# Where the gate read-back, the first weight tiles and the first gathers stand in the queues of a product-key expert layer

## The chip, the cores and the metric

The kernel runs on one core of a Trainium2 chip. The metric is device time in microseconds (us) of one launch, the median of the runs shown. TensorE is PE, VectorE is DVE, ScalarE is ACT, GpSimd is POOL, SyncE is SP; each takes its instructions in program order.

## What is computed

A decoder trunk of two layers on 512 tokens of width 1024. A layer is an attention mixer of four head groups and, behind it, an expert sub-layer of 16,384 experts, on which the change works:

```python
s1 = einsum('thd,kd->thk', q[:, :, 0], sub_k1); s2 = einsum('thd,kd->thk', q[:, :, 1], sub_k2)
v1, i1 = top_k(s1, 16); v2, i2 = top_k(s2, 16)
top_s, top_j = top_k(v1[..., :, None] + v2[..., None, :], 16)
eid = take_along_axis(i1 * 128 + i2, top_j); gate = softmax(top_s)
act = gelu(einsum('cd,ced->ce', h, u[eid]))          # 8 heads x 16 experts a token
out = einsum('ce,ced->cd', gate * act, v[eid])
x = x + g2 * out
```

## The kernel before

The 512 tokens are four tiles of 128. For the first three tiles the expert sub-layer is done densely: all 16,384 experts, in 128 blocks of 128, are multiplied on PE with 384 tokens, and a matrix of gates, zero nearly everywhere, picks the chosen ones. The fourth tile is done sparsely: for each of its 128 (head, rank) pairs a gather on POOL fetches one row of `peer_u` or `peer_v` a token, and DVE makes the dot product or the weighted sum.

Every dense product is made of three matmuls, since each operand is split into a high part (ACT copies it, rounded) and a low part (DVE or POOL subtracts). For block e these are `uh`, `ul` (from the load `ur`), `vh`, `vl` (from `vr`), and for the gated activations `wdh`, `wdl`.

The sub-layer of a layer has two stages.

**The planned stage** is put in order by `Plan`, a list scheduler with costs and due times, which writes one instruction order for each engine. It does the search for the largest scores, decodes the chosen expert numbers (`ids`, `places`, `chosen`, `decoded`, `finish`: tiles `cid`, `oh`, `ts`), and turns gates into dense blocks: DVE writes one-hot tiles `o` (L1656), scales them by the high and low part of the gates into `og` (L1669 on DVE, or L1666 on ACT for the low part, as the plan chooses), PE multiplies them (L1677), ACT evacuates into `gs` (L1683), and SP stores `gs` to DRAM as `gdram` (L1686). The u products of the first blocks run in between (`u_mm`, PE L204 to L206 on `psb`), each followed by a Gelu into a ring of `act` tiles. `QD` gives the due times of the four tiles' decoding; the fourth tile's decoding ends in `eid` and `g3`, which only the gathers and their weights need.

**The loop** over e is written by hand (from L1908 on), in the order of the code. Step e loads `ur` of block e + 33 and `vr` of block e + 3, reads back a quarter of a `gq` tile every fourth step (the gates of four blocks out of `gdram`), multiplies act by gates (`w_mul`), splits (`w_split`, `v_split`), runs `u_mm(e + 31)` and then `products(e)`, 18 matmuls into `psa`. Between them come about three uses of gathered tiles on DVE (`g_use`, L1795 and L1800), each followed by the next gather on POOL (`g_issue`, L1775). `GB` = 6 gather buffers, three buffers of `vr` and three of `ur` are in turn.

Ahead of the loop, in this order: six gathers are issued; then `v_load` of blocks 0, 1 and 2, `gq_load(0)`, `v_split(0)`, and `prepare(0)`, which is `w_mul(0)` and `w_split(0)`. PE's first product of the loop, `products(0)`, so waits for `gq`, `act`, `wdh` and `wdl` of block 0.

Of the kernel before, what the change touches and what calls it, by code (L numbers as in the profile page):

```python
# [30 lines left out]
LA = 3  # L31
PE_EPS = 0.05
SAME = 0.1
QD = (30, 70, 110, 150, 2)
GD = (45, 2.4)
UD = (0, 6.2)
QS = ((0, 30), (30, 30), (60, 34))
# [12 lines left out]
URB, VRB, GB = 3, 3, 6  # L50
# [102 lines left out]
def trunk(ctx: ExitStack, tc: tile.TileContext, I, out):  # L153
# [514 lines left out]
    for l in range(L):  # L668
# [113 lines left out]
        with tc.tile_pool(name=f"hP{l}", bufs=1) as hp, tc.tile_pool(name=f"U{l}", bufs=1) as up:  # L782
            state = peer(nc, tc, I, l, xd, fh, fl, h3, (order, qcm, hcm, ocm), q0, (wq0, wq1, wq2), both, wq_mm, right, hp, up, small, bank, mm3, iota128, cst["pos"], ident, dram, grow,
                         (ada_load, ada_mac, ada_finish, [(l, 5)] + [(l + 1, j) for j in range(2 if l + 1 < L else 0)]), l + 1 < L, lambda l=l: rows_out(l + 1))
# [543 lines left out]
def peer(nc, tc, I, l, xd, fh, fl, h3, closing, q0, w012, both, wq_mm, right, hp, up, small, bank, mm3, iota128, pos, ident, dram, grow, ada, more, rows_out):  # L1328
    V, S, G, PE, SY = nc.vector, nc.scalar, nc.gpsimd, nc.tensor, nc.sync
# [41 lines left out]
    def act_room():  # L1371
        return ring[0].tile([128, 384], F32, name="act", tag="act", bufs=RING + 1)
# [4 lines left out]
    with tc.tile_pool(name=f"Q{l}", bufs=1) as qp:  # L1377
# [7 lines left out]
        raw, w, qcs, q1, jps, tops, cands, cms = {}, dict(enumerate(w012)), {}, {}, {}, {}, {}, []  # L1385
# [178 lines left out]
        if True:  # L1564
            picked, cids, ohs, prs, turned = {}, {}, {}, {}, {}

            def weigh(i):
                tf = wp.tile([128, 16, 8], F16, name="tf", tag="tf", bufs=2)
                V.tensor_copy(tf, tj[:, i].rearrange("p h s -> p s h"))
                ge = wp.tile([128, 8, 16], F32, name="ge", tag="ge", bufs=2)  # L1570
                V.tensor_tensor(out=ge, in0=ts[:, i], in1=bc(ts[:, i, :, 0:1], [128, 8, 16]), op=ALU.subtract)
                picked[i] = (tf, ge)
# [117 lines left out]
            for i in range(NT):  # L1690
                due, d = B0 + QD[i], QD[4]
                head = t = plan.add(due, lambda i=i: weigh(i), ("W", 0.35), after=[lg[h, i] for h in range(8)] + [ready], take=("p",))
# [74 lines left out]
    def g_issue():  # L1767
        nonlocal issued
        if issued < len(events):
            kind, s = events[issued]  # L1770
            t = ep.tile([128, D], F32, name="gt", tag="gt", bufs=GB)
            if kind == "a":
                ada[0](*s, t)
            else:
                G.indirect_dma_start(out=t, out_offset=None, in_=I["peer_u" if kind == "u" else "peer_v"],  # L1775
                                     in_offset=bass.IndirectOffsetOnAxis(ap=eid3[:, s:s + 1], axis=0))
            gtile[issued] = t
            issued += 1
# [30 lines left out]
            V.tensor_mul(w3[:, r], w3[:, r], g3[:, r])  # L1809
            wdone += 1  # L1810

    for _ in range(GB):
        g_issue()

    with tc.tile_pool(name=f"D{l}", bufs=1) as dp, ExitStack() as order:
        acc = [None] * 6
        vraw, vspl, wspl, gq = {}, {}, {}, {}
# [1 line left out]
        def v_load(e):  # L1819
            if e < 128:  # L1820
                vraw[e] = up.tile([128, D], F32, name="vr", tag="ur", bufs=URB) if e >= 126 else dp.tile([128, D], F32, name="vr", tag="vr", bufs=VRB)
                SY.dma_start(vraw[e], I["peer_v"][(l * 128 + e) * 128:(l * 128 + e + 1) * 128, :])

        def gq_load(q):
            if q < 32:
                gq[q] = dp.tile([128, NTG, 4, TG], F32, name="gq", tag="gq", bufs=2)
                SY.dma_start(gq[q], gdram[:, :, 4 * q:4 * q + 4, :].rearrange("g p a t -> p g a t"))

        def w_mul(e):
            w = acts[e].rearrange("p (g t) -> p g t", g=NTG)  # L1830
            V.tensor_mul(w, w, gq[e // 4][:, :, e % 4, :])

        def w_split(e):
            w = acts.pop(e)
            if e >= 126:
                t = up.tile([128, D], F32R, name="wd", tag="ur", bufs=URB)
                wh, wl = t[:, :384], t[:, 384:768]
            else:
                wh, wl = (dp.tile([128, 384], F32R, name=q, tag=q, bufs=2) for q in ("wdh", "wdl"))
            S.activation(wh, w, AF.Copy)  # L1840
            V.tensor_sub(wl, w, wh)  # L1841
            wspl[e] = wh, wl

        def v_hi(e):
# [9 lines left out]
        def prepare(e):  # L1854
            w_mul(e)
            w_split(e)

        def v_split(e):
            v_hi(e)
            v_lo(e)  # L1860
# [37 lines left out]
        def x_add(i):  # L1898
            V.tensor_add(xs[i], xs[i], a3)

        early = {107: [(v_load, 126)], 108: [(v_load, 127)], 109: [(x_load, 3), (lambda i: grow(l, i), 5)], 110: [(v_hi, 126)], 111: [(v_lo, 126)], 112: [(v_hi, 127)], 113: [(v_lo, 127)],
                 115: [(x_mul, 3)], 116: [(x_add, 3)], 119: [(gq_load, 31)], 120: [(w_mul, 126)], 121: [(w_split, 126)], 122: [(w_mul, 127)], 123: [(w_split, 127)]}
        if more:
            for q in range(3):
# [1 line left out]
                    early.setdefault(98 + q + 3 * n, []).append((f, q))  # L1906

        order.enter_context(tc.manual_schedule())  # L1908
        for e in range(3):
            v_load(e)  # L1910
        gq_load(0)
        v_split(0)
        prepare(0)
        def a_load(e):
            acts[e] = act_room()
            SY.dma_start(acts[e], adram[e - NU])

        for e in range(125):
            if e + RING + 2 < NU:
                u_load(e + RING + 2)  # L1920
            if NU <= e + AD < 128:
                a_load(e + AD)
            if e < 123:
                v_load(e + 3)
            if e % 4 == 1 and e < 120:
                gq_load(e // 4 + 1)
            if e + RING - 1 < NU:
                u_act(e + RING - 1)
            prepare(e + 1)
            if e + RING + 1 < NU:  # L1930
                u_hi(e + RING + 1)
                u_lo(e + RING + 1, V)
            v_split(e + 1)
            for f, n in early.get(e, ()):
                f(n)
            if e + RING < NU:
                u_mm(e + RING)
            if e < 124:
                for i in range(3):
                    products(i, (e,), False)  # L1940
            upto = min(len(events), (e + 1) * len(events) // PACE)
            while used < upto:
                g_use()
                g_issue()
                g_weights()
# [195 lines left out]
```

## Time and profile before

| | |
|---|---|
| median of 3 runs | 3256.21 us (3254.5 to 3257.57) |
| the profiled execution | 3257.48 us, span of its trace 3255.7 us |
| PE busy | 3118.8 us, 96% of the span |
| DVE busy | 2576.4 us, 79% |
| ACT, POOL busy | 1329.4 us (41%), 856.1 us (26%) |
| mean granted TensorE clock | 0.984 of full speed |

The span runs from the first to the last instruction; the execution's own time has 1.8 us more around it. Busy shares are means over stages with different limits, so what one stage costs is read from its own waits.

### The profile page before, as it was taken

To read this page: it belongs to the slowest core of one execution; us is meant where nothing else is said; L and a number is where in the kernel's file an instruction comes from. 1 tells how busy PE (TensorE), PEld (TensorE's weight loads), DVE (VectorE), ACT (ScalarE), POOL (GpSimd) and SP (SyncE) were. 2 spreads that over 40 slices of the span, in tenths; PEclk is the share of its full clock that TensorE was granted. 3 is DMA by queue.
4 is the path that set the end of the run, shared out by engine and by line. 5 is a ranking of instruction groups with operands and counts; after the bars stand their busy time and mean duration, and the time that the engine had idled before them with its cause. 6 is when DMAs were issued, how large, how long until landed. Compare 5 with 4: busy or idle time off the path is not lost.

```text
span 3255.7 us, 47426 instructions
## 1 busy us (share of the span) xinstructions
PE 3118.8 (96%) x17316; PEld 2709.0 (83%) x17316; DVE 2576.4 (79%) x5530; ACT 1329.4 (41%) x2485; POOL 856.1 (26%) x694
## 2 busy tenths in 40 slices
PE   6999999989999999999989999998999999999998
PEld 5876877779989999998889678787899899999987
DVE  7757799978888888786666868999687778878856
ACT  3268414643333333333442864246333333333333
POOL 1300220024433343341022003100333444444400
PEclk9999999989999999999999999999999999999999
DMA  8502214679989999896654032146888899999954
GB/s 280 157 9 78 106 58 157 233 289 337 333 316 340 325 331 348 313 355 217 203 180 144 4 125 85 53 182 245 302 326 327 325 323 326 323 326 322 322 185 159
DMA packets 291339, 762.73 MB, mean 234 GB/s; under 512 B 23832, under 2 KB 130968, under 8 KB 285984
## 3 DMA queue, kind: packets, MB, share of 16 engines
q1 hardware_dynamic: 217376, 491.22, 43.5%
q0 software_dynamic: 73728, 268.47, 22.4%
q8 instruction: 136, 2.23, 0.3%
q14 instruction: 99, 0.81, 0.1%
HBM read 700.86 MB, written 58.74 MB: 233 GB/s over the span
## 4 chain that ended last, share of the span: by engine, by line
PE 72%; DVE 19%; DMA 4%; ACT 3%; issue 2%; POOL 0%; SPq 0%; DVEq 0%; POOLq 0%; ACTq 0%
PE psa L205 12%; PE psa L206 12%; PE psa L204 12%; PE psb L204 9%; PE psb L206 9%; PE psb L205 9%; DVE o L1656 2%; DVE og L1669 2%; PE psa L864 2%; DVE s L1457 1%; DMA wr<-in_w_in 1%; PE psa L897 1%; DMA gq<-gdram 1%; DVE ki L1455 1%; PE psa L1677 1%
## 5 line engine op out<-in xcount | busy, mean ns | idle before, releaser
L206 PE MATMUL psb<-bh,ul 128*128 128x384 f32 x1824 | 615.4, 337 | 5.2 <-DVE ul L1356 5.2
L204 PE MATMUL psb<-bh,uh 128*128 128x384 f32 x1824 | 618.6, 339 | 0.9 <-DVE arow L251 0.9
L205 PE MATMUL psb<-bl,uh 128*128 128x384 f32 x1824 | 613.5, 336 | 0.0
L204 PE MATMUL psa<-vh,wdh 128*128 128x512 f32 x1512 | 589.9, 390 | 14.5 <-ACT wdh L1840 14.5
L206 PE MATMUL psa<-vh,wdl 128*128 128x512 f32 x1512 | 593.4, 392 | 0.0
L205 PE MATMUL psa<-vl,wdh 128*128 128x512 f32 x1512 | 593.1, 392 | 0.0
L1775 POOL DMA_INDIRECT gt<-in_peer_u,eid x256 | 334.5, 1307 | 669.3 <-DVE gt L1795 235.4
L1840 ACT ACTIVATE wdh<-act 128x384 fp32r<-128x384 f32 x252 | 132.2, 524 | 866.5 <-PE psa L205 629.2
L1775 POOL DMA_INDIRECT gt<-in_peer_v,eid x256 | 324.6, 1268 | 428.3 <-DVE a L1800 199.6
L1841 DVE TENSOR_TENSOR wdl<-act,wdh 128x384 fp32r<-128x384 f32 x252 | 141.0, 559 | 284.9 <-ACT wdh L1840 274.9
L204 PEld LDWEIGHTS psb<-bh,uh 128*128 128x128 f32 x1824 | 345.0, 189 | 11.0 <-DVE arow L251 2.7
L205 PEld LDWEIGHTS psb<-bl,uh 128*128 128x128 f32 x1824 | 344.8, 189 | 8.1
L206 PEld LDWEIGHTS psb<-bh,ul 128*128 128x128 f32 x1824 | 344.3, 189 | 6.8 <-DVE ul L1356 6.8
L1356 DVE TENSOR_TENSOR ul<-ur,uh 128x1024 fp32r<-128x1024 f32 x222 | 271.9, 1225 | 91.6 <-ACT uh L1353 76.1
L204 PEld LDWEIGHTS psa<-vh,wdh 128*128 128x128 f32 x1512 | 285.1, 189 | 70.1 <-ACT wdh L1840 15.1
L206 PEld LDWEIGHTS psa<-vh,wdl 128*128 128x128 f32 x1512 | 284.6, 188 | 59.9
L205 PEld LDWEIGHTS psa<-vl,wdh 128*128 128x128 f32 x1512 | 284.6, 188 | 55.7
L1852 DVE TENSOR_TENSOR vl<-vr,vh 128x1024 fp32r<-128x1024 f32 x252 | 307.7, 1221 | 23.1 <-ACT vh L1849 22.7
L1800 DVE SCALAR_TENSOR_TENSOR a<-gt,w,a 128x1024 f32<-128x1024 f32 x254 | 325.2, 1280 | 0.8
L1795 DVE SCALAR_TENSOR_TENSOR gt<-gt,h 128x1024 f32<-128x1024 f32 x256 | 310.5, 1218 | 0.0
L1376 ACT ACTIVATE act<-psb 128x384 f32<-128x384 f32 x256 | 125.8, 491 | 394.9 <-PE psb L206 335.6
L1353 ACT ACTIVATE uh<-ur 128x1024 fp32r<-128x1024 f32 x228 | 238.7, 1047 | 91.7 <-PE psb L205 61.9
(389 smaller groups left out, 5285.7 us busy)
## 6 DMA issues: line engine op xcount, KB each, us to landing
ur<-in_peer_uT SPq DMA_DIRECT2D x256, 512.0 KB
vr<-in_peer_v SPq DMA_DIRECT2D x256, 512.0 KB
gdram<-gs SPq DMA_DIRECT2D x24, 2048.0 KB
gq<-gdram SPq DMA_DIRECT2D x64, 768.0 KB
O<-in_ada_w SPq DMA_DIRECT2D x48, 512.0 KB
gt<-in_ada_w SPq DMA_DIRECT2D x32, 512.0 KB
wr<-in_w_q SPq DMA_DIRECT2D x14, 1024.0 KB
wr<-in_w_out SPq DMA_DIRECT2D x16, 512.0 KB
```

Of the source, the lines that this page charges most:

```text
L204: PE.matmul(ps, lhsT=wh, rhs=mh, start=first, stop=False)
L205: PE.matmul(ps, lhsT=wh, rhs=ml, start=False, stop=False)
L206: PE.matmul(ps, lhsT=wl, rhs=mh, start=False, stop=last)
L1353: S.activation(uspl[e][0], uraw[e], AF.Copy)
L1356: eng.tensor_sub(uspl[e][1], uraw.pop(e), uspl[e][0])
L1376: S.activation(acts[e], ups.pop(e)[:, :384], AF.Gelu_apprx_tanh)
L1775: G.indirect_dma_start(out=t, out_offset=None, in_=I["peer_u" if kind == "u" else "peer_v"], in_offset=bass.IndirectOffsetOnAxis(ap=eid3[: ...
L1795: V.scalar_tensor_tensor(t, t, 1.0, h3, op0=ALU.mult, op1=ALU.mult, accum_out=d3[:, s:s + 1])
L1800: V.scalar_tensor_tensor(a3, t, w3[:, s:s + 1], a3, op0=ALU.mult, op1=ALU.add)
L1840: S.activation(wh, w, AF.Copy)
L1841: V.tensor_sub(wl, w, wh)
L1852: V.tensor_sub(vspl[e][1], vraw.pop(e), vspl[e][0])
```

## The change

Three edits, in both layers. The six first gathers are issued behind `prepare(0)` instead of ahead of the first loads. `gq_load(0)` stands behind the first `v_load` instead of the third, and `v_load` of blocks 1 and 2 follow `prepare(0)`. In `w_split(0)` the low part is subtracted on POOL instead of DVE. And the due time of the fourth tile's decoding goes from 150 to 170.

```diff
-QD = (30, 70, 110, 150, 2)
+QD = (30, 70, 110, 170, 2)
...
-    for _ in range(GB):
-        g_issue()
-
...
             S.activation(wh, w, AF.Copy)
-            V.tensor_sub(wl, w, wh)
+            (V if e else G).tensor_sub(wl, w, wh)
...
         order.enter_context(tc.manual_schedule())
-        for e in range(3):
-            v_load(e)
+        v_load(0)
         gq_load(0)
         v_split(0)
         prepare(0)
+        for e in range(1, 3):
+            v_load(e)
+        for _ in range(GB):
+            g_issue()
```

Lines behind L1812 of the kernel before stand three lower in the changed one. PE's instructions are the same, in the same order.

The first place is DVE at the end of the planned stage, first layer (`o`, `og`: one-hot tiles and scaled ones; `cid`, `oh`, `ts`: decoding of the fourth tile; `ul`: low part of a u block). Before:

```order
L1669 TENSOR_TENSOR og<-o,gT 128x1024 x4
L1656 TENSOR_TENSOR o<-iota_5065,iT 128x2048 x2
L1669 TENSOR_TENSOR og<-o,gT 128x1024
L1595 TENSOR_TENSOR oh<-oh,cid 128x1120
L1669 TENSOR_TENSOR og<-o,gT 128x1024
L1589 TENSOR_TENSOR oh<-tf,pos_5067 128x1600
L1669 TENSOR_TENSOR og<-o,gT 128x1024
L1601 TENSOR_TENSOR oh<-oh 128x544
L1601 TENSOR_TENSOR oh<-oh 128x288
L1603 TENSOR_REDUCE ts<-oh 128x8x4
L1595 TENSOR_TENSOR oh<-oh,cid 128x1600
L1356 TENSOR_TENSOR ul<-ur,uh 128x1024
```

And now, the same place:

```order
L1656 TENSOR_TENSOR o<-iota_5065,iT 128x2048 x2
L1669 TENSOR_TENSOR og<-o,gT 128x1024 x4
L1656 TENSOR_TENSOR o<-iota_5065,iT 128x2048 x2
L1669 TENSOR_TENSOR og<-o,gT 128x1024 x4
L1356 TENSOR_TENSOR ul<-ur,uh 128x1024
L1580 TENSOR_TENSOR cid<-ifl 128x128
L1580 TENSOR_TENSOR cid<-ifl 128x64
```

The last `og` was one of three on DVE, with the fourth on ACT; now all four are DVE's, the seven `cid` of L1580 with a fold and a reduction, and the first two of `oh` shown, stand behind it, and another `ul` (not shown) has moved ahead. The whole decoding now stands ahead of the third `ul` and of `eid`. On ACT two of the four last groups of eight L1666 are gone.

The second place is SP's queue where the loop begins, first layer (`ur`, `vr`: u and v blocks; `gdram`: store of gates; `gq`: their read-back). Before:

```order
L1686 DMA gdram<-gs 128x4096 x2
L1345 DMA ur<-in_peer_uT 128x1024
L1686 DMA gdram<-gs 128x4096
L1345 DMA ur<-in_peer_uT 128x1024 x2
L1822 DMA vr<-in_peer_v 128x1024 x3
L1827 DMA gq<-gdram 128x12x128
L1345 DMA ur<-in_peer_uT 128x1024
L1822 DMA vr<-in_peer_v 128x1024
```

Now:

```order
L1686 DMA gdram<-gs 128x4096 x2
L1345 DMA ur<-in_peer_uT 128x1024
L1686 DMA gdram<-gs 128x4096
L1345 DMA ur<-in_peer_uT 128x1024
L1819 DMA vr<-in_peer_v 128x1024
L1824 DMA gq<-gdram 128x12x128
L1819 DMA vr<-in_peer_v 128x1024 x2
L1345 DMA ur<-in_peer_uT 128x1024
```

One `ur` has moved ahead of the last three stores, and the read-back stands behind one `vr` instead of three.

The third place is POOL where the loop begins, first layer (a piece of the difference: `wdl` is the low part of the gated activations of block 0, `gt` a gathered tile):

```order
 L1559 CAST pos_5067<-consts 128x904
 L1356 TENSOR_TENSOR ul<-ur,uh 128x1024 x3
+L1838 TENSOR_TENSOR wdl<-act,wdh 128x384
 L1775 DMA gt<-in_peer_u,eid_3863 128x1024 x17
 L1775 DMA gt<-in_peer_v,eid_3863 128x1024
```

POOL does one subtraction ahead of the first gather, and since it takes its instructions in order the six gathers now wait for it, and so for `gq`. On DVE `w_mul(1)` then follows `w_mul(0)` directly.

## Rows read from the trace of the kernel before

**Rows 1.** The page, busy time, share of the span and instructions of each engine.

```profile
PE 3118.8 (96%) x17316; PEld 2709.0 (83%) x17316; DVE 2576.4 (79%) x5530; ACT 1329.4 (41%) x2485; POOL 856.1 (26%) x694
```

**Rows 2.** Waits of PE, whole span: us in total, times, longest.

```profile
PE psa L204 <- ACT wdh L1840: 14.5, 2, 7.6
```

**Rows 3.** Timeline of PE, first layer: start, us, instruction, [idle before, releaser].

```profile
675.00 0.67 PE L204 MATMUL psb<-bh,uh 128*128 128x384 f32 x1
...
703.93 0.80 PE L204 MATMUL psa<-vh,wdh 128*128 128x512 f32 x1 [6.94 <-ACT wdh L1840]
...
709.50 0.40 PE L205 MATMUL psa<-vl,wdh 128*128 128x512 f32 x1
709.73 0.39 PE L206 MATMUL psa<-vh,wdl 128*128 128x512 f32 x1
```

**Rows 4.** Timeline of PE, second layer, first product of the loop.

```profile
2311.45 0.80 PE L204 MATMUL psa<-vh,wdh 128*128 128x512 f32 x1 [7.56 <-ACT wdh L1840]
```

**Rows 5.** Busy time by stretches: PE, PEld, DVE, ACT, POOL, PEclk, DMA share, GB/s.

```profile
704.00:707.00 3.00, 3.00 (x7) 2.44 (x8) 2.02 (x4) 2.28 (x4) 0.00 (x0) 0.50 0.24 97
...
1100.00:1300.00 200.00, 200.00 (x1021) 182.30 (x1019) 162.61 (x203) 69.93 (x99) 80.33 (x62) 1.00 0.90 330
```

**Rows 6.** The chain that ended last, around 685 us: start, us, what.

```profile
685.48 17.26 DMA gq<-gdram
```

**Rows 7.** Timeline of SP's queue, first layer: start, us to issue.

```profile
675.91 0.32 SPq L1686 DMA_DIRECT2D gdram<-gs  x1
...
684.16 1.28 SPq L1822 DMA_DIRECT2D vr<-in_peer_v  x3
```

**Rows 8.** DMA queues from 692 to 694 us: packets, MB, share of 16 engines.

```profile
q0 software_dynamic: 174, 0.64, 83.7%
q1 hardware_dynamic: 174, 0.09, 18.8%
```

**Rows 9.** DMA queues from 712 to 713 us (the loop's second `gq`).

```profile
q1 hardware_dynamic: 551, 0.28, 99.8%
```

**Rows 10.** Timeline of DVE, first layer, end of the plan and first steps.

```profile
654.72 0.77 DVE L1580 TENSOR_TENSOR cid<-ifl 128x128 int16<-128x128 int16 x7
...
656.38 2.35 DVE L1656 TENSOR_TENSOR o<-iota,iT 128x2048 f16<-128x2048 f16 x2
...
668.81 0.73 DVE L1595 TENSOR_TENSOR oh<-oh,cid 128x1120 int16<-128x1120 int16 x1
...
670.07 0.98 DVE L1589 TENSOR_TENSOR oh<-tf,pos 128x1600 int16<-128x1600 f16 x1
670.97 0.68 DVE L1669 TENSOR_TENSOR og<-o,gT 128x1024 f16<-128x1024 f16 x1
...
676.72 1.21 DVE L1356 TENSOR_TENSOR ul<-ur,uh 128x1024 fp32r<-128x1024 f32 x1
...
690.96 1.23 DVE L1852 TENSOR_TENSOR vl<-vr,vh 128x1024 fp32r<-128x1024 f32 x1
...
709.90 1.22 DVE L1795 SCALAR_TENSOR_TENSOR gt<-gt,h 128x1024 f32<-128x1024 f32 x1
...
713.23 1.23 DVE L1356 TENSOR_TENSOR ul<-ur,uh 128x1024 fp32r<-128x1024 f32 x1 [0.40 <-ACT uh L1353]
```

**Rows 11.** Timeline of ACT, first layer, its last work of the gate blocks.

```profile
672.49 2.43 ACT L1666 ACTIVATE og<-o,gL 128x128 f16<-128x128 f16 x8
```

**Rows 12.** Groups of instructions, shapes apart: busy us, mean ns, idle before.

```profile
L1841 DVE TENSOR_TENSOR wdl<-act,wdh 128x384 fp32r<-128x384 f32 x252 | 141.0, 559 | 284.9 <-ACT wdh L1840 274.9 <-PE psa L206 8.7 <-issue 0.7
L1437 POOL TENSOR_TENSOR hw<-fh,fl 128x384 f32<-128x384 f32 x16 | 19.3, 1240 | 18.5 <-PE psa L762 18.5
```

**Rows 13.** Timeline of POOL, first layer: the first and the seventh gather.

```profile
685.10 1.17 POOL L1775 DMA_INDIRECT gt<-in_peer_u,eid  x1 [74.74 <-DMA ur<-in_peer_uT]
...
710.25 1.68 POOL L1775 DMA_INDIRECT gt<-in_peer_u,eid  x1 [17.26 <-DVE gt L1795]
```

**Rows 14.** DMA queues from 688 to 690 us.

```profile
q0 software_dynamic: 4, 0.02, 2.0%
```

## Prediction

> **What bounds the kernel now.** Ask first which engine is full. By the page's busy row it is PE, 96% of the span [rows 1], and in the middle of the first layer's loop PE is busy 200 us of 200 at full clock, with DVE at 162.6 us and the DMA engines at 0.90 [rows 5]. An edit gains there only by taking work from PE, and this one leaves PE's instructions alone. What remains are PE's own waits. The list of them has one entry with few, long waits: ACT's `wdh` holds `psa` back twice, 14.5 us together [rows 2]. The timeline puts them ahead of `products(0)` of each layer, 6.94 us at 703.93 in the first [rows 3], 7.56 us at 2311.45 in the second [rows 4]. So the edit, which stands at just this place, aims at the two largest stalls.
>
> Who is late? The chain that ended last goes through `gq`: issued at 685.48, underway for 17.26 us, landed at 702.7 [rows 6]; behind it come `w_mul(0)` on DVE and `wdh` on ACT. The DMA view says why it takes so long: between 692 and 694 us the gathers' queue moves 174 packets and `gq`'s queue also 174, but 0.64 against 0.09 MB [rows 8]. The two queues take turns packet by packet, a gather's packet is 4 KB and one of `gq` 512 bytes. So `gq` creeps until the six gathers (3.1 MB, issued from 685.10 [rows 13]) are through. When a later `gq` runs by itself its queue moves 551 packets, 0.28 MB, in 1 us [rows 9]; the whole tile (0.79 MB) then takes 2.8 us.
>
> The wait costs more than its length. In 704 to 707 us PE is busy throughout but the granted clock is 0.50, the lower level of 1.2 GHz [rows 5]; 17 of the 18 matmuls of `products(0)` take from 703.93 to 709.73, 5.80 us [rows 3]. Where matmuls follow each other without a gap one begins 0.23 us behind the one before (709.50 and 709.73 [rows 3]), so 17 take 3.9 us at full clock. Slow clock: 1.9 us a layer.
>
> **The due time.** On DVE three pieces of decoding stand ahead of the last `og`: from 654.72 to 656.38 (1.66 us), 0.73 and 0.98 us, 3.4 us [rows 10]; I take 3.2, as neighbours overlap a little. They go behind it. In exchange a `ul` (1.2 us) and two `og`, which ACT did, come ahead; `og` to `og` is about 0.6 us, so 2.4 in all. DVE's last `og` begins about 0.8 us before 670.97, at 670.2, and ends near 670.7. ACT's eight small `og` (672.49, 2.43 us [rows 11]) are gone, so ACT is no longer last. PE's last gate matmuls follow in 1.0 to 1.9 us: PE's next u block, at 675.00 now [rows 3], begins at 671.9 to 672.9. Gain 2.1 to 3.1, I take **2.5 us**. The last store, at 675.91 [rows 7], goes at about 672.7.
>
> The cost lies on DVE. Its whole decoding now stands ahead of the third `ul`. What follows the last `og` took at most from 671.6 to 676.72 (5.1 us, [rows 10]); with 3.2 us more and a `ul` it ends at 670.7 + 1.2 + 8.3 = 680.2 at the latest. PE comes to that `ul` two u blocks into its run, near 681.3 (two of some 4.2 us, and two matmuls), so I cost it at nothing; the cover is about 1 us, and each us beyond it is lost.
>
> **The read-back.** SP's `vr` loads were issued at 684.16, 8.2 us behind the last store [rows 7], as they wait for its landing. Now they can go at 672.7 + 8.2 = 681, or at the decoding's end: `vr` at 681.7, `gq` at 682.1. Ahead of it in its queue are one `ur` and one `vr`, 1.05 MB. The two queues together moved 0.73 MB in 2 us [rows 8], so 2.9 us; then 2.8 for `gq`, and some 0.5 of latency: `gq` lands at **688.3**. If its packets still shared with `vr` of blocks 1 and 2 (another 1.05 MB, 2.9 us) it would be 691.
>
> DVE's `vl` of block 0 at 690.96 [rows 10] moves with its inputs to 688.5 and ends at 689.7; `w_mul(0)`, at most 0.6 us, by 690.3; `wdh` on ACT by 690.9. `wdl` moves to POOL. No row has that operation there. On DVE it takes 559 ns, the nearest of its size on POOL 1240 ns [rows 12]: 0.56 is the floor and 1.24 the nearest shape, a subtraction from the same kind of tiles, which I take; at twice that all would still be ready by 693.4. So `products(0)` can begin at **692.2**. When does PE want it? At 703.93 - 6.94 = 697.0 now, at 694.5 with the first edit. Cover 2.3 us, 0 to 3.6 with the bounds above: the waits and, as PE then never stops, the slow clock are gone.
>
> **The gathers.** They are issued behind `wdl`, at 692.2 instead of 685.10, so 7 us later. Who waits? `g_use` on DVE, and behind it in DVE's order the `ul` of step 2 and 3, for which PE waits. Issued at 685.10, the gathers have moved only 4 packets by 690 [rows 13, 14]: 4.8 us to start. At 0.64 MB in 2 us beside the other queue [rows 8] one gather (0.52 MB) takes 1.6 us. Gather 0 is there near 692.2 + 4.8 + 1.6 + 1 of latency = 699.6, gather 1 at 701.2; with its dot product of 1.22 us [rows 10] DVE is through with both near 702.8. The `ul` of the second step is 3.3 us behind a dot product (709.90 to 713.23 [rows 10]), and ends 1.2 us later. PE wants it 3 steps of 4.16 us (18 matmuls at 0.23) and two matmuls into the loop: 694.5 + 12.5 + 0.3 = 707.3. The latest harmless end of the second dot product is therefore some 703.9: cover **1.1 us**. After that DVE is slack, 162.6 of 200 us [rows 5].
>
> A gather's own instruction is now issued beside a working DVE. The seventh, which is, took 1.68 us, the first, beside an idle DVE, 1.17 [rows 13]; the 0.5 us stands in the times above. Here a rule speaks against the change. The Trainium skill, "SBUF — State Buffer", section "SBUF: two separate sides", says that GpSimd cannot write a gather's descriptors while VectorE runs an operation in a mode that takes the shared port pair. By the rule each gather could be held back for a whole DVE operation, and the time would be that of the rival "late gathers" below; by the row, half a microsecond, the sum. The profile's row does not settle which, since that gather was issued between DVE's operations or beside them, and the row doesn't tell.
>
> **Sum.** The waits, 14.5, plus 2 × (2.5 + 1.9) = 23.3 us. The profiled execution is 3257.5 us, so 3234.2; it lies 1.3 above the median of 3256.2, so **3233 us**.
>
> **Rivals.**
> - *Late gathers.* Each is held by a DVE operation of 1.2 us: the second comes 2.4 us later, 1.3 us beyond the cover. PE stalls 1 to 4 us a layer in steps 2 to 4, and the slow clock takes its 1.9 us there. Lost 2 × 3.2, so 3239; 3236 to 3246. For it: the small cover and six gathers behind one operation. Against it: 0.5 us in the row, and a DVE that has pauses while it waits for gathers.
> - *The change doesn't do it.* `gq` stays late since it stands behind the last store's 8.2 us and the longer decoding, and not behind the gathers. It has to land by some 691; every us beyond is lost, twice. At 693 to 697 the time is 3240 to 3254, with the clock lost too: 3245 to 3256. For it: the 17.26 us are long and only two stretches of them were read. Against it: equal packets in both queues, which is what sharing looks like.
> - *The gathers become the small share.* Behind `vr`, `ur` and `gq` of the loop, issued without pause, the gathers arrive as late as `gq` did. The cover of 11.5 us a layer (2.5 + 6.94 + 1.9, plus the 1.1) is used up when gather 1 lands at about 713, 21 us behind its issue; then the time is that of before, and at 24 us 3262. For it: `gq`'s own 17.26 us. Against it: the gather's packets are the large ones where two queues take turns, and 0.90 of the DMA engines is demand that leaves room.
>
> **How the numbers follow.** Forecast 0.69, its own range 3229 (the first edit at 3.1, fewer small waits) to 3237 (2.1, `ul` 1 us late in each layer); late gathers 0.17; no effect of the read-back 0.10, of which about half ends within 0.2% (6.5 us, about what a measurement of this kernel can tell from no change); the slow gathers 0.04. Faster 0.69 + 0.17 + 0.04 = 0.90, same 0.06, slower 0.04. For 8 in 10 the range takes the forecast's and most of the late gathers': 3228 to 3245.
>
> **What would show it.** Right: PE's wait for `wdh` is gone in both layers; the granted clock at `products(0)` is 1.00; `gq` is underway some 6 us; the u block behind the gates begins about 2.5 us earlier; POOL's first gather stands behind `wdl`; DVE has a new wait of 1 to 3 us for a gathered tile with no wait of PE behind it. Wrong: PE waits for `ul`, at the third u block (the decoding was too long) or in steps 2 to 4 (late gathers), or still for `wdh`, with `gq` issued later than 684 or underway over 10 us.

## The result, and the profile after

The changed kernel takes 3229.44 us (median of 4 runs, 3229.25 to 3230.57), the kernel before 3255.36 us beside it (4 runs): ratio 0.992, 95% interval 0.9903 to 0.9937, 25.9 us less where 23 were forecast. Medians here and below leave out two runs near 3867 us, at a granted clock of 0.75, one of the kernel before and one of an experiment. The profiled execution of the changed kernel took 3229.47 us, with a span of 3227.7 us; the span of before was 28.0 us longer.

The list of PE's waits, whole span (us in total, times, longest), no longer has the entry for `wdh` of [rows 2]:

```profile
PE psa L1677 <- DVE og L1669: 22.4, 22, 2.0
...
PE psb L206 <- DVE ul L1356: 5.3, 3, 2.6
```

PE's timeline of the changed kernel shows the first layer's last gate matmuls, the u block behind them, `products(0)`, the `ul` matmul of u block 33, and then the second layer's u block and `products(0)`:

```profile
667.62 3.41 PE L1677 MATMUL psa<-og,o 128*128 128x128 f16 x31 [0.97 <-DVE og L1669]
670.79 0.58 PE L204 MATMUL psb<-bh,uh 128*128 128x384 f32 x1
...
691.84 0.39 PE L204 MATMUL psa<-vh,wdh 128*128 128x512 f32 x1
692.07 0.40 PE L205 MATMUL psa<-vl,wdh 128*128 128x512 f32 x1
...
704.62 0.34 PE L206 MATMUL psb<-bh,ul 128*128 128x384 f32 x1
...
2263.96 0.67 PE L204 MATMUL psb<-bh,uh 128*128 128x384 f32 x1
...
2285.43 0.39 PE L204 MATMUL psa<-vh,wdh 128*128 128x512 f32 x1
```

No bracket stands behind `products(0)` in either layer, and its matmuls follow each other every 0.23 us from the first on, where those of [rows 3] began slowly. The view by stretches says the same of the clock (sixth group of numbers: the granted clock):

```profile
668.00:671.00 3.00, 3.00 (x30) 3.00 (x28) 2.96 (x12) 1.79 (x3) 0.00 (x0) 0.50 0.21 49
...
671.00:673.00 2.00, 2.00 (x13) 2.00 (x13) 1.97 (x4) 0.60 (x1) 0.00 (x0) 0.97 0.81 332
...
690.00:693.00 3.00, 3.00 (x18) 2.79 (x17) 2.73 (x3) 2.31 (x3) 2.45 (x3) 1.00 0.91 305
```

The last gate matmuls still run at half clock, the u block behind them nearly at full. In the kernel before, the first 2 us of that u block were slow as well (8 matmuls instead of 13):

```profile
675.00:677.00 2.00, 2.00 (x8) 2.00 (x7) 1.90 (x6) 0.89 (x2) 0.00 (x0) 0.50 0.43 106
```

SP's queue, changed kernel, the lines that answer to [rows 7] and the start of `gq`:

```profile
671.69 0.32 SPq L1686 DMA_DIRECT2D gdram<-gs  x1
...
679.03 0.33 SPq L1819 DMA_DIRECT2D vr<-in_peer_v  x1
679.42 0.43 SPq L1824 DMA_DIRECT2D gq<-gdram  x1
679.90 2.25 SPq L1819 DMA_DIRECT2D vr<-in_peer_v  x2
```

DVE, the lines that answer to [rows 10]: its last `og`, `w_mul` of blocks 0 and 1, two dot products, and the `ul` of block 33:

```profile
665.69 2.49 DVE L1669 TENSOR_TENSOR og<-o,gT 128x1024 f16<-128x1024 f16 x4
...
688.01 1.03 DVE L1828 TENSOR_TENSOR act<-act,gq 128x384 f32<-128x384 f32 x2 [0.82 <-DMA gq<-gdram]
...
695.55 1.23 DVE L1795 SCALAR_TENSOR_TENSOR gt<-gt,h 128x1024 f32<-128x1024 f32 x1 [2.29 <-DMA gt<-in_peer_u,eid]
...
698.53 1.23 DVE L1795 SCALAR_TENSOR_TENSOR gt<-gt,h 128x1024 f32<-128x1024 f32 x1 [1.75 <-DMA gt<-in_peer_u,eid]
...
701.86 1.22 DVE L1356 TENSOR_TENSOR ul<-ur,uh 128x1024 fp32r<-128x1024 f32 x1 [0.39 <-ACT uh L1353]
```

POOL, the lines that answer to [rows 13]:

```profile
689.21 1.01 POOL L1838 TENSOR_TENSOR wdl<-act,wdh 128x384 fp32r<-128x384 f32 x1 [81.43 <-ACT wdh L1837]
690.40 1.27 POOL L1775 DMA_INDIRECT gt<-in_peer_u,eid  x1 [0.18 <-issue]
```

`gq`, issued at 679.42, is on DVE at 688.01: 8.6 us underway instead of 17.26. `wdl` is ready at 690.22, 1.6 us ahead of PE. The gathers start 11 us behind `gq`, and DVE has the new waits for them, 2.29 and 1.75 us, that PE doesn't feel.

**Where the time came from.** PE's instructions are the same in both kernels, so distances between the same instructions can be compared. Below they are worked out from PE's timelines in each layer: from the first matmul of L1369 (in the planned stage, ahead of everything that the change moves) to the u block behind the gates, from there to the start of `products(0)`, and from there to the start of `products(20)`.

| kernel | layer 1: to u block, `products(0)`, `products(20)` | layer 2: the same |
|---|---|---|
| before | 197.2, 28.9, 168.0 | 196.3, 30.5, 168.1 |
| changed | 195.7, 21.1, 166.1 | 195.2, 21.5, 166.1 |
| changed, again (`e9_again`) | 195.2, 21.3, 166.1 | 195.5, 21.2, 166.1 |
| due time alone (`e1_due_only`) | 194.4, 29.4, 168.0 | 194.6, 29.0, 168.0 |
| order of loads alone (`e8_order_only`) | 196.7, 22.4, 166.3 | 196.1, 21.5, 166.1 |
| held gathers alone (`e7_hold_only`) | 196.6, 22.3, 167.6 | 197.2, 23.8, 168.7 |
| due time and order (`e2_low_on_dve`) | 195.5, 21.1, 166.1 | 194.0, 20.9, 166.1 |
| due time and hold (`e3_old_loads`) | 194.1, 23.3, 168.0 | 193.8, 21.4, 168.4 |
| order and hold (`e4_old_due`) | 196.4, 22.8, 166.1 | 196.2, 22.6, 166.1 |

The changed kernel gains 1.6 + 7.9 + 1.9 us in the first layer and 1.1 + 9.0 + 2.0 in the second (worked out before rounding), together 23.5, against 23.3 forecast. The 1.9 and 2.0 are `products(0)` at full clock: from its first to its eighteenth matmul it takes 3.9 us instead of the 5.80 of [rows 3].

The spans differ by 28.0 us. The other 4.6 lie where no edit stands, 2.6 us ahead of L1369 in the first layer and 1.9 between `products(20)` of the first layer and L1369 of the second, and such stretches differ between two profiles of one kernel too. The first matmul of L1369 in the first layer, for the kernel before:

```profile
477.76 0.81 PE L1369 MATMUL psb<-hw,ur 128*128 128x384 f32 x2
```

For the changed kernel:

```profile
475.12 0.81 PE L1369 MATMUL psb<-hw,ur 128*128 128x384 f32 x2
```

And for the same kernel profiled again (`e9_again`):

```profile
481.45 0.81 PE L1369 MATMUL psb<-hw,ur 128*128 128x384 f32 x2
```

The two profiles of one kernel are 6.3 us apart here, and 2.9 us in the stretch between the layers. Of the kernel before there is one profile, so a small part of the rest may still be the change's; that stays open. In the experiments below, where the kernel before took 3247 to 3263 us in single runs, what a median gives and what the distances give differ by up to 4 us either way; the edits are judged by the distances.

### The profile page after: what moved, and what is told of

The parts are those of the page before. It is cut to its first block, busy times and chain, and to the rows that moved or that the text cites. A ratio compares the mean times of both kernels' runs of the same rounds, so it can differ in the third digit from the quotient of the medians.

```text
span 3227.7 us, 47400 instructions
## 1 busy us (share of the span) xinstructions
PE 3105.7 (96%) x17316; PEld 2697.9 (84%) x17316; DVE 2577.1 (80%) x5532; ACT 1319.0 (41%) x2453; POOL 859.0 (27%) x696
## 3 DMA queue, kind: packets, MB, share of 16 engines
q0 software_dynamic: 73728, 268.47, 22.6%
q8 instruction: 136, 2.23, 0.3%
## 4 chain that ended last, share of the span: by engine, by line
PE 72%; DVE 20%; DMA 3%; ACT 3%; issue 2%; POOL 0%; SPq 0%; DVEq 0%; POOLq 0%; ACTq 0%
PE psa L205 12%; PE psa L206 12%; PE psa L204 12%; PE psb L204 9%; PE psb L206 9%; PE psb L205 9%; DVE og L1669 2%; DVE o L1656 2%; PE psa L864 2%; DVE s L1457 1%; PE psa L897 1%; DMA wr<-in_w_in 1%; DVE ki L1455 1%; PE psa L1677 1%; DVE ki L1461 1%
```

## The experiments

Theories at the start: **A**, the read-back is late because its small packets take turns with the gathers' large ones; **B**, because three `vr` loads stood ahead of it; **C**, because the last store was late.

**The due time alone**, the kernel before with

```diff
-QD = (30, 70, 110, 150, 2)
+QD = (30, 70, 110, 170, 2)
```

> The kernel before with the fourth tile's decoding due at 170, and nothing else. Theory A (the read-back is late because its small packets take turns with the gathers' large ones; the due time is worth only its own shift and the stretch of slow clock behind the gate blocks, 2.2 us in the first layer and 2.5 in the second): the last store, the loads, the read-back and the gathers all move earlier together, PE still waits 6 to 8 us for wdh in each layer, and the time falls by 4 to 5 us, to about 3251 (3249 to 3253). Theory C (the read-back is late because the last store is, so the due time pays for the wait): the wait shrinks by more than half and the time falls to 3245 or below.

Measured: 3246.67 us beside 3255.3 (ratio 0.9972, 0.996 to 0.9984). PE's wait is all there, 7.14 us in the first layer (6.93 in the second):

```profile
707.01 0.79 PE L204 MATMUL psa<-vh,wdh 128*128 128x512 f32 x1 [7.14 <-ACT wdh L1840]
```

and the DMA queues (packets, MB, share of 16 engines) of 696 to 698 us show packet for packet what [rows 8] did:

```profile
q0 software_dynamic: 195, 0.71, 87.5%
q1 hardware_dynamic: 197, 0.10, 17.0%
```

C is out: store, loads, `gq` and gathers all moved earlier together. By the table the due time is worth 1.8 us a layer up to the u block (the four kernels with the old one have a mean of 196.7 and 196.4, the five with the new one 195.0 and 194.6). Behind it, up to `products(0)` and without its wait, the kernels with the new due time and an edit of the queues take 20.9 to 21.5 us, those with the old due time 21.5 to 22.9. That piece of about 1 us can't be put down to the due time: with the due time alone the stretch takes 22.2 and 22.1 us, about as in the kernel before (22.0 and 22.9), and the u block starts at half clock:

```profile
677.60:680.00 2.40, 2.40 (x10) 2.40 (x9) 2.37 (x7) 0.67 (x2) 0.00 (x0) 0.50 0.81 306
```

The fall of the clock comes at another point of the gate blocks in this profile; what decides it is open. The median lies below A's range; the distances, 226.2 to 223.8 us in the first layer and 226.8 to 223.6 in the second, give 5.6 us.

**The gathers not held**, the changed kernel with

```diff
-            (V if e else G).tensor_sub(wl, w, wh)
+            V.tensor_sub(wl, w, wh)
```

> The changed kernel with the low part of block 0's gated activations subtracted on DVE again, so that nothing holds the gathers on POOL; the order of the loads and the due time stay changed. Theory A: the gathers are issued within 2 us of the read-back instead of 10 us behind it, the read-back is caught by them half way and lands at 693 to 697 us, PE waits 3 to 6 us for wdh in each layer and takes another 1.8 us at slow clock: 3229.4 + 2 x (3 + 1.8) to 3229.4 + 2 x (6 + 1.8), so 3239 to 3245. Theory B (the read-back was late because three vr loads stood ahead of it; the order of the loads pays): the time of the changed kernel, 3229 to 3231.

Measured: 3229.76 us beside 3255.3 (0.9916, 0.9903 to 0.993), the time of the changed kernel. A as it stood falls. The first gather is issued at 682.91, 0.5 us behind `gq`; yet `gq` is on DVE 10.3 us behind its issue:

```profile
692.70 0.56 DVE L1828 TENSOR_TENSOR act<-act,gq 128x384 f32<-128x384 f32 x1 [2.48 <-DMA gq<-gdram]
```

The DMA view of 685 to 687 us says why. The gathers have been issued, but their queue has no packet yet, and the queue of `gq` and the weight loads has the engines for itself:

```profile
q1 hardware_dynamic: 657, 0.57, 89.5%
```

(657 packets of 512 bytes would be 0.34 MB; about 65 of these are of 4 KB, from the loads.) So the gathers harm only what is left of `gq` when they begin to move, here between 687 and 689 us and so over 4 us behind their issue, much as [rows 13, 14] had it. Call this **A2**.

**The old order of the loads**, the changed kernel with

```diff
-        v_load(0)
+        for e in range(3):
+            v_load(e)
         gq_load(0)
         v_split(0)
         prepare(0)
-        for e in range(1, 3):
-            v_load(e)
```

> The changed kernel with the read-back behind all three vr loads again; the gathers still wait on POOL and the due time stays changed. Theory A: two more vr loads are ahead, 1.05 MB or about 3 us at the rate of the queue; the read-back lands near 690 instead of 688, PE waits 0 to 2 us for wdh in each layer: 3230 to 3235. Theory B: the read-back comes as late as before, PE waits 5 to 7 us in each layer and runs slow behind it: 3243 to 3248.

Measured: 3232.97 us beside 3255.3 (0.9931, 0.9918 to 0.9945), in A's range. B falls as the main cause. With the gathers held, two more loads ahead cost a wait of 2.23 us in the first layer and 0.27 in the second:

```profile
697.64 0.70 PE L204 MATMUL psa<-vh,wdh 128*128 128x512 f32 x1 [2.23 <-ACT wdh L1837]
...
2292.53 0.50 PE L204 MATMUL psa<-vh,wdh 128*128 128x512 f32 x1 [0.27 <-ACT wdh L1837]
```

**The old due time**, the changed kernel with `QD` back at 150.

> The changed kernel with the fourth tile's decoding due at 150 again; gathers and loads as changed. Theory A: it gives back the shift of the due time and the slow clock behind the gate blocks, 2.2 and 2.5 us; no wait for wdh of more than 1 us: 3232 to 3236, and with the run of the due time alone the two parts add up. Theory C: the read-back is late again with the last store, and PE waits over 3 us for wdh in each layer: 3241 or more.

Measured: 3237.47 us beside 3255.3 (0.9946, 0.9932 to 0.996), and no wait for `wdh`. Some 8 us are given back by the medians, above A's range; by the table's sums it is 2.5 and 2.2, about what A had.

**Each of the two edits of the queues by itself.** The first, on the kernel before:

```diff
-    for _ in range(GB):
-        g_issue()
...
-            V.tensor_sub(wl, w, wh)
+            (V if e else G).tensor_sub(wl, w, wh)
...
         prepare(0)
+        for _ in range(GB):
+            g_issue()
```

> The kernel before with the gathers behind block 0's preparation and its low part on POOL; due time and order of the loads as before. Theory A2 (the read-back has to be through before the gathers begin to move, which is 5 us behind their issue; holding the gathers or calling the read-back earlier does either of it): PE waits 0 to 2.5 us for wdh in each layer, 3235 to 3241. Rival (both edits of the queues are needed together): waits of 4 us or more, 3243 or more.

The second, also on the kernel before:

```diff
-        for e in range(3):
-            v_load(e)
+        v_load(0)
         gq_load(0)
         v_split(0)
         prepare(0)
+        for e in range(1, 3):
+            v_load(e)
```

> The kernel before with the read-back behind one vr load instead of three; due time, gathers and subtraction as before. Theory A2: the read-back lands 9 to 10 us behind its issue, just ahead of or among the first gathers, PE waits under 1 us for wdh in each layer, 3233 to 3239. Rival (both edits of the queues are needed together): waits of 4 us or more, 3243 or more.

Measured: the hold alone 3238.92 us beside 3255.2 (0.9947, 0.9926 to 0.9967), with one wait for `wdh`, of 1.75 us in the second layer; the order alone 3233.77 us (0.9939, 0.9917 to 0.996), with none. Either edit takes nearly all of the wait, which is A2: calling `gq` ahead of two `vr` lets its packets pass before most of the gathers' do, and holding the gathers lets them pass as well.

In time they are not equal. By the table's sums the order alone gains 20 us of the 23.5, the hold alone 13. Behind three `vr` `gq` takes 9.1 to 11.5 us to reach DVE even with the gathers held (kernels `e3_old_loads` and `e7_hold_only`), behind one 7.7 to 8.6, so theory B has a small share. The held gathers are then late themselves: with the hold alone PE waits for `wdl` and again for u block 33. In the second layer:

```profile
2294.36 0.50 PE L204 MATMUL psa<-vh,wdh 128*128 128x512 f32 x1 [1.75 <-ACT wdh L1837]
...
2295.45 0.50 PE L206 MATMUL psa<-vh,wdl 128*128 128x512 f32 x1 [0.35 <-POOL wdl L1838]
...
2308.32 0.45 PE L204 MATMUL psb<-bh,uh 128*128 128x384 f32 x1 [0.64 <-ACT uh L1353]
...
2309.58 0.44 PE L206 MATMUL psb<-bh,ul 128*128 128x384 f32 x1 [0.64 <-DVE ul L1356]
```

Such waits are most of why this kernel's third distance is 167.6 and 168.7 us where the changed kernel's is 166.1. With the order and the due time changed, the hold adds nothing: the kernel without it has the time of the changed one.

**Wide packets.** If taking turns is what hurt, `gq` should bear the gathers with larger packets, all else as in the run of the due time:

```diff
-    gdram = dram.tile([NTG, 128, 128, TG], F32, ...)
+    gdram = dram.tile([128, 32, NTG, 4, TG], F32, ...)
...
-                SY.dma_start(gdram[tg], gst.pop(tg))
+                SY.dma_start(gdram[:, :, tg], gst.pop(tg).rearrange("p (q a) t -> p q a t", a=4))
...
-                SY.dma_start(gq[q], gdram[:, :, 4 * q:4 * q + 4, :].rearrange("g p a t -> p g a t"))
+                SY.dma_start(gq[q], gdram[:, q])
```

> The kernel before with the due time of 170, loads and gathers as before, and the gates laid out in DRAM so that a read-back finds 6 KB in a row for each partition, where it found twelve pieces of 512 bytes; the stores are cut into 512-byte pieces in exchange. Theory A (the read-back's small packets get a small share beside the gathers' 4 KB packets): the share grows to about a half, the read-back is underway 10 to 12 us instead of 17, PE waits 0 to 2 us for wdh in each layer instead of 7: 3246.7 less 2 x (5 to 7) less 2 x 1.8 of slow clock, 3229 to 3233, and up to 6 us more if the stores land later. Theory D (the gathers were simply first, and their 3.1 MB have to pass whatever the packets are): underway 15 us or more, PE waits as before, 3243 or more.

Measured: 3235.16 us beside 3255.2 (0.9945, 0.9923 to 0.9967), within the 6 us that A left for later stores: the last store but one landed 9.5 us behind its issue, 6.7 in the run of the due time. From 686 to 688 us both queues again move equal numbers of packets, but `gq`'s queue now moves the larger part of the bytes:

```profile
q1 hardware_dynamic: 82, 0.47, 57.4%
q0 software_dynamic: 82, 0.34, 42.2%
```

`gq` is underway 10.0 us (681.27 to 691.28) and 8.9 us in the second layer, and PE waits 1.03 and 1.04 us instead of 7. That is as fast as behind the same three `vr` with the gathers held. The gathers and the loads' order were those of before, and the stores, the one other thing that differs, don't move beside the gathers: the packet size makes the difference, and D is out.

**Gathers held longer**, the changed kernel with

```diff
             (V if e else G).tensor_sub(wl, w, wh)
+            if e == 0:
+                for _ in range(4):
+                    G.tensor_sub(dp.tile([128, 384], F32R, name="jk", tag="jk", bufs=1), w, wh)
```

> The changed kernel with four more subtractions of the same kind (into a tile that nobody reads) on POOL between the low part of block 0 and the first gather, 1.0 us each, so that the gathers are issued about 4 us later. By the changed kernel's trace the ul of u block 33 ends 1.5 us ahead of the matmul that needs it. Theory L (late gathers are paid for beyond that cover): PE waits 2 to 3 us for ul in each layer and runs 1.8 us longer at slow clock behind the wait, 3229.4 + 2 x 4.3 = 3238 (3234 to 3241). Rival (DVE has slack in the loop and catches up before PE needs it): no wait of over 0.5 us, 3228 to 3232.

Measured: 3243.15 us beside 3255.2 (0.9958, 0.9944 to 0.9973), 13.7 more than the changed kernel and above L's range. The four subtractions took 6.34 us, not 4. The second dot product ended 14.0 us behind the start of `products(0)` in place of 7.9, 6.1 us later, and PE stood at u block 33 for 4.1 us (4.8 in the second layer), with half the clock behind it (0.50 from 2309 to 2312 us in the second layer):

```profile
712.92 0.45 PE L204 MATMUL psb<-bh,uh 128*128 128x384 f32 x1 [3.50 <-ACT uh L1353]
...
714.18 0.69 PE L206 MATMUL psb<-bh,ul 128*128 128x384 f32 x1 [0.64 <-DVE ul L1356]
```

Late gathers are paid for, with a cover near 2 us (6.1 less 4.1); the changed kernel stays within it. ACT is named, but its `uh` only waited behind `wdh(1)`, and that for DVE's dot products.

**The changed kernel again, and fewer `og` on DVE.** As DVE's `og` are what PE waits for now, two kernels move some to ACT by the planner's cost, 2.0 and 1.6 in the place of 2.4:

```diff
-... [("W", 0.602), ("G", 2.3), ("S", 2.4)][:LA], after=(hi,))
+... [("W", 0.602), ("G", 2.3), ("S", 2.0)][:LA], after=(hi,))
```

> The changed kernel once more, unaltered, beside the two below and on their chip. Nothing of the change touches PE's work ahead of the last gate blocks, so what differs there between two profiles is not the change's: the start of PE's matmuls in the first layer's planned stage (469 us in the changed kernel's profile) lies anywhere within 1.5 us ahead and 7.5 us behind, as in the eight runs so far, and the time at 3228 to 3236.

> The changed kernel with the planner's cost of the low part of a scaled tile on ACT at 2.0 instead of 2.4, which moves 36 groups of eight small og from DVE to ACT, 18 a layer, so 18 x 0.6 = 10.8 us less for DVE and 18 x 2.4 = 43 us more for ACT in each layer. If DVE is what PE waits for at the end of the planned stage (22.4 us of waits for og, 11 a layer) the time falls by 4 to 12 us, to 3218 to 3226. Rival (ACT's small og then are last, as the one ahead of the last store was in the kernel before, and the evacuations queue behind them): same or slower, 3229 to 3240.

> The same with the cost at 1.6: 58 groups moved, 29 a layer, 17 us less for DVE and 70 us more for ACT in each layer. If DVE bounds: 3215 to 3224. Rival (ACT is last): slower than with the cost at 2.0, 3232 to 3250.

Measured beside 3256.45 us: again 3230.58 (0.9925, 0.9902 to 0.9948), cost 2.0 3233.62 (0.9935, 0.9913 to 0.9956), cost 1.6 3251.42 (0.9988, 0.9975 to 1.0). The start of L1369 in the kernel run again lies 6.3 us later, within what was expected. PE's waits for DVE's `og` do shrink, 22.5 to 16.8 and 13.6 us, but nothing is won. With 2.0 ACT's timeline has small `og` ahead of the last evacuations again, as [rows 11] had:

```profile
672.01 2.43 ACT L1666 ACTIVATE og<-o,gL 128x128 f16<-128x128 f16 x8
674.35 1.54 ACT L1683 ACTIVATE gs<-psa 128x512 f32<-128x512 f32 x3
...
679.66 0.58 ACT L1683 ACTIVATE gs<-psa 128x512 f32<-128x512 f32 x1
```

The rival holds for 1.6, with a time 1 us above its range. Whether 2.0 is worth or costs a little can't be told from these runs: up to `products(20)` it takes 1.7 us less in the first layer and 1.3 more in the second. None of the versions is clearly faster than the changed kernel; the one with `wdl` on DVE equals it.

## Why the prediction came out right

- **The wait for `wdh`** (14.5 us): gone in both layers, as forecast. The cause given, equal packets of unequal size in two queues, is shown by the wide read-back. What the prediction didn't see is that either of the two edits of the queues takes nearly all of the wait: it put the gain down to both together, and costed the move to POOL as something needed. It also called these the two largest stalls. The list of before has a longer one at the start of the program, which the change doesn't touch:

```profile
PE psa L305 <- DVE RST L300: 12.3, 1, 12.3
```

- **The due time** (2.5 us a layer up to the u block): mis-sized, 1.6 and 1.1 us between these two profiles, 1.8 over all. DVE's last `og` came where it was put (its end at 668.18, which is 670.8 on the clock of before, as the stage began 2.6 us earlier; forecast 670.7). The term that was off is PE's tail behind it, "1.0 to 1.9 us", for which no row was given: 31 matmuls were still to do and PE was at half clock, so it took 2.6. (670.7 and that tail give 671.7 to 672.6, where 671.9 to 672.9 stands.) The longer decoding, costed at nothing, cost nothing: PE has no wait for `ul` ahead of `products(0)`.
- **The slow clock** (1.9 us a layer at `products(0)`): 1.9 and 2.0. A second piece was missed: the u block behind the gates also ran slow before and hardly does now, 0.9 and 1.5 us. This surplus of 2.4 us and the 2.3 us that the due time fell short cancel. That the steps add up so well is luck to this extent.
- **The read-back** (landing at 688.3): issue right (682.1 forecast, 682.1 on the clock of before), flight mis-sized, 8.6 us for 6.2. It did share with `vr` of blocks 1 and 2 (from 685 to 687 us their queue moved 526 packets, 0.73 MB, where packets of 512 bytes alone would be 0.27); the text's other value, 691, is what came (690.6). `wdl` on POOL took 1.01 us, between the bounds. The cover was 1.6 us, not 2.3. The 0.5 and 1 us of latency in the sums come from no row, and no run here shows them by themselves.
- **The gathers**: the second dot product ended at 702.4 on that clock, 702.8 forecast; the `ul` of block 33 ended 1.5 us ahead of its matmul at 704.62 (1.1 forecast). The steps to it were off and cancelled. "4.8 us to start" was read from the kernel before; in the changed one, issued at 690.40, the gathers' queue has no packet up to 692 us and 83 in the next 2 us, so they started some 2 us behind their issue, and the first needed longer to land. Why the start takes 2 us in one kernel and over 4 in another is open. From 692 to 694 us:

```profile
q0 software_dynamic: 83, 0.34, 66.8%
```

- **A gather's issue beside DVE**: the prediction read the first gather of [rows 13] as issued beside an idle DVE. It was not; a `ul` ran beside it, and beside the seventh, by [rows 10], the dot product at 709.90:

```profile
685.47 1.22 DVE L1356 TENSOR_TENSOR ul<-ur,uh 128x1024 fp32r<-128x1024 f32 x1 [2.94 <-ACT uh L1353]
```

  So the rows did tell that an issue can be slow beside one operation and not beside another. The rule of the Trainium skill that was weighed ("SBUF — State Buffer", section "SBUF: two separate sides") did not decide the time: the first six issues took 0.94 to 1.85 us here, and none cost PE anything.
- **The rivals**: late gathers cost PE time where they were held 6 us longer, and a little where they were held with the read-back still behind three `vr`, but not in the changed kernel. "The change doesn't do it" and the slow gathers did not come. Their prices were off: by the cover of 691 a landing at 693 to 697 gives 3237 to 3245, and 3241 to 3249 with the clock; and 2.5 + 6.94 + 1.9 is 11.3, with the 1.1 12.4, where 11.5 stands.

The median, 3 to 4 us below the forecast and at the edge of its own range, is not explained by these steps, whose sum agrees within 0.5 us. In the profiles the rest lies where no edit stands and where two profiles of one kernel differ as much; that it is no part of the change is likely, and not shown.

## What to carry to other kernels

Before a slow transfer is blamed on its bytes or its place, read packets and bytes of both queues in its stretch: equal counts with unequal sizes mean that the one with small packets gets little, and here larger packets, an earlier issue and a later rival each took most of the wait away. Where two edits cure one wait, undo each alone before crediting either, and follow PE past the wait: the later rival gave some of it back further on. And count the clock with every gap: the waits of 6.94 and 7.56 us cost 8.8 and 9.5.

## What the hardware showed that was not expected

Subtractions on POOL and DVE slowed each other. Of the four extra subtractions on POOL those beside a working DVE took 1.33 to 1.88 us, the last, with DVE idle, 1.02; beside them DVE's `ul` and `vl` took 1.69 and 2.03 us in place of 1.22 (kernel with gathers held longer):

```profile
695.32 1.69 DVE L1356 TENSOR_TENSOR ul<-ur,uh 128x1024 fp32r<-128x1024 f32 x1 [0.27 <-ACT uh L1353]
696.94 2.03 DVE L1852 TENSOR_TENSOR vl<-vr,vh 128x1024 fp32r<-128x1024 f32 x1
```

A gather's issue beside such a subtraction of DVE, on the other hand, was not slow (0.96 us at 691.98, changed kernel); one beside a dot product was (1.85 us at 695.73). Over the whole trace of the changed kernel the 192 issues that overlap most with a `scalar_tensor_tensor` of DVE have a median of 1.68 us, the 320 beside a `tensor_tensor` or an idle DVE one of 0.94.

And not every wait was followed by a lower clock: behind one of 1.03 us it was 1.00 over the next 3 us (wide read-back), behind one of 2.23 us it was 0.53 (old order of the loads). Two cases don't say what decides it.

```profile
692.50:695.50 3.00, 3.00 (x13) 2.28 (x14) 2.02 (x4) 2.29 (x4) 0.00 (x0) 1.00 1.03 414
...
697.60:700.60 3.00, 2.96 (x6) 1.90 (x7) 1.92 (x3) 3.00 (x5) 2.45 (x3) 0.53 0.04 18
```
